# Low parts of the input weights by an accumulating DMA instead of a subtraction on GpSimd

## Chip, cores and metric

One core of a Trainium2 chip runs the whole program. The metric is the device time in microseconds; three runs of the kernel before took 576.79, 578.21 and 579.08 us, median 578.21.

## What is computed

The reference is one layer of a hybrid encoder on 1024 tokens of 1024 channels, float32:

```python
hn = rms_norm(h, ln_g)
proj = hn @ w_in + b_in                      # 1024 x 3584
glu_a, glu_b, z_conv, q, k, v, z_att = split(proj, 7 parts of 512)
y_conv = conformer_conv(glu_a, glu_b, ...)   # GLU, depthwise conv of width 31, LayerNorm, swish, pointwise
y_att = neighbourhood_attention(q, k, v, rpb)  # 8 heads of 64, 16 x 64 grid, window 8 x 16
y_conv = grouped_rms_norm(y_conv, gn_conv_g) * silu(z_conv)
y_att = grouped_rms_norm(y_att, gn_att_g) * silu(z_att)
out = rms_norm(h + concat(y_conv, y_att) @ w_out, final_g)
```

## The kernel before

Every large product is made from operands in two parts: the high part is the value rounded to float32r, the low part is what the rounding left. A product is then three matmuls, high by high, high by low and low by high (lines 384 to 386). For the input projection the weight is the stationary operand. It is cut into 28 chunks of 128 output channels; a chunk is one tile of 128 partitions by 8 parts (k) by 128 columns, 512 KB, and serves two halves of 512 tokens, 24 matmuls each.

`prefetch` (line 337) brings the chunks in the order of the work: the chunks of the GLU (b0, a0, b1, a1, b2, a2), then q0, k0, v0 make the lead (`LEAD`); the rest (`FILL`) is woven with the attention; the convolution gate's c3 and the attention gate's a3 come last, in `final_gates` (line 1033). For each chunk SyncE loads the raw weight into the one raw buffer (`wraw`, line 210); when one of two high/low buffer pairs is free, ScalarE copies the raw weight into `whi` in two pieces of four parts, which rounds it (line 351), and GpSimd subtracts: `wlo = raw - whi` (`low_weight`, line 355), also in two pieces. A pair is given back (`r_w.put`) when the second half of its chunk has been issued, so the pair of chunk n goes to chunk n + 2. The raw buffer is given back after the last subtraction.

All engines issue in the order in which this program was built. The class `Clock` plans that order: streams of work are generators that give the time from which they can go on, and queues of ScalarE, VectorE and GpSimd are booked with a cost for each instruction. Jobs for GpSimd wait in `ck.jobs` and are written when its booked queue is free (line 114). `proj` (line 368) takes a chunk's part k when its booked ready time has come, and other streams are taken meanwhile where they have work. In `final_gates` the products go part by part, c3 and then a3, so that every part lets go of its normalised input, whose buffers then take the output projection's operands.

VectorE works the 31 taps of the depthwise convolution through (`taps`, line 470), each a product and sum of two tiles in SBUF, and between them the low parts of q and k (`ql`, `kl`), which read the PSUM bank that the next projection needs. GpSimd has besides the subtractions the small powers of the norms and the attention's scalings, in order on one queue.

Of the kernel before, what the change touches and what calls it, by code (L numbers as in the profile page):

```python
# [32 lines left out]
CH_A, CH_B, CH_ZC, CH_Q, CH_K, CH_V, CH_ZA = 0, 4, 8, 12, 16, 20, 24  # L33
# rows of the small-vector tile
V_LN, V_BIN, V_DWB, V_CLG, V_CLB, V_GNC, V_GNA, V_N = 0, 8, 36, 40, 44, 48, 52, 56
# column blocks of 16 queries: (first 8-column granule, granules, bias class)
BLK = [(0, 3, 0), (1, 4, 1), (3, 4, 1), (5, 3, 2)]
BW = [24, 32, 24]
# row halves: (first key row, key rows)
HF = [(0, 11), (4, 12)]  # L40
# [30 lines left out]
class Ring:  # L71
    """the buffers of a tag, by the time from which each is free"""

# [16 lines left out]
class Clock:  # L90
    """Every engine issues in the order of this program. The work comes as streams, generators that give the
    time from which they can go on; they are woven by a clock of the tensor engine and of the others' queues."""

# [55 lines left out]
def block(ctx: ExitStack, tc: tile.TileContext, x, vecs, w_in, dw_w, pw_w, pw_b, rpb, w_out, final_g, out):  # L149
# [41 lines left out]

# [1 line left out]
    warm = const.tile([P, 1], F32, name="warm")  # L193
# [4 lines left out]

# [1 line left out]
    acc = yp.tile([P, NC4, T], F32, name="acc")  # L200
# [4 lines left out]

    # chunks of the projection in the order of the work: glu, q, k and v, gates of the attention and of the convolution
    of = {"g": (CH_B, CH_A), "q": (CH_Q,), "k": (CH_K, CH_V), "a": (CH_ZA,), "c": (CH_ZC,), "p": ()}
    order = [c + int(f[1:]) for f in LEAD + FILL for c in of[f[0]]] + [CH_ZC + 3, CH_ZA + 3]

    def wraw(n):  # L210
        c = order[n]
        raw = wrp.tile([P, NK, P], F32, tag="wr", name=f"wr{c}")
        nc.sync.dma_start(out=raw, in_=w_in[0][:, c * P:(c + 1) * P].rearrange("(k p) n -> p k n", p=P))
        return raw
# [66 lines left out]
    def turned(h):  # L281
        """first the banks of several chunks at a time, so that each tile of x is turned as it comes"""
        todo_ = list(range(NK))
        for group in ((("tr", "tr", "s", "s", "o", "ln"),) if h == 0 else ()) + (("tr",), ("s",)) * NK:
            ks, todo_ = todo_[:len(group)], todo_[len(group):]
            pts = []
            for k, tag in zip(ks, group):
                yield from RB[tag].get()
                pts.append((k, tag, bank(tag, f"px{h}_{k}", NB[tag])))
            for j in range(4):  # L290
                t = 4 * h + j
                while t not in x_ready:
                    yield ck.now + 0.1
                if x_ready[t] + ck.HOP > ck.now:
                    yield x_ready[t] + ck.HOP
                for k, tag, pt in pts:
                    ck.tp(pt[:, j * P:(j + 1) * P], xt[t][:, k * P:(k + 1) * P], ident)
                    if j == 3:
                        sl = slice(512 * h, 512 * h + 512)
                        e = ck.act(out=hi[k][:, sl], in_=pt, func=AF.Copy, scale=col(V_LN + k))  # L300
                        ck.spawn(low(h, k, pt, sl, e, RB[tag]), -1)
            yield
        for _ in range(4):
            r_u.put()
# [22 lines left out]

# [1 line left out]
    ready = {}  # L329

    def split(raw, whi, wlo, after=None, eng="pool"):
        """hi and lo of a weight; gives the time"""
        t = ck.act(after, out=whi, in_=raw, func=AF.Copy)
        k = dict(out=wlo, in0=raw, in1=whi.bitcast(F32), op=ALU.subtract)
        return ck.gps("tensor_tensor", 0.1 + 0.0022 * size(raw), t, **k) if eng == "pool" else ck.dve("tensor_tensor", t, **k)

    def prefetch():
        for n in range(len(order)):
            if n < W_AHEAD or "pw" in state:
                yield from r_raw.get()  # L340
                raw, end = (wraw(n), ck.now + 4.0) if n else (raw0, land_w)
                yield from r_w.get()
            else:
                yield from r_w.get()
                yield from r_raw.get()
                raw, end = wraw(n), ck.now + 4.0
            whi, wlo = wtiles(n)
            yield end
            for k0 in range(0, NK, KS):
                kk = slice(k0, k0 + KS)  # L350
                t = ck.act(out=whi[:, kk, :], in_=raw[:, kk, :], func=AF.Copy)
                ck.jobs.append((t, partial(low_weight, n, raw, whi, wlo, kk)))
                yield

    def low_weight(n, raw, whi, wlo, kk):
# [12 lines left out]
    def proj(w, h, name, order=None, tag="pj"):  # L368
        """one chunk of channels for half of the tokens; order: width of the column blocks
        that become the outer dimension of the tokens"""  # L370
        whi, wlo, wt = w
# [18 lines left out]

# [1 line left out]
    # CLS: first query row, first key row written, key rows, window by the row offsets -4..3  # L392
    CLS = ((0, 0, 8, False), (4, 0, 11, True), (8, 4, 12, True), (12, 8, 8, False))
# [3 lines left out]
    def bias_rows():  # L397
# [20 lines left out]
        r_gz.put()  # L418
        # a window that moves with the column: columns c0..c0+n, bias columns from 7 on
        for t, c0, n in ((0, 8, 8), (1, 0, 16), (2, 0, 9)):  # L420
            w = BW[t]
            for h in range(8):
# [3 lines left out]
                yield ck.now + 0.3  # L426
        # a window at the border
        for t, start, cs in ((0, 0, range(8)), (2, 8, range(9, 16))):
            for c in cs:
                nc.sync.dma_start(out=ab[t][:, c, :, start:start + 16], in_=rp8[:, :, 15 - c:31 - c])  # L430
                yield ck.now + 0.3
        # a row of mask before, and laid out for the query rows
        for t in range(3):
# [31 lines left out]

# [1 line left out]
    # a sigmoid is half of 1 + tanh of the half, and the taps carry the half  # L467
    u, conv_end = [], [0.0] * 8
# [21 lines left out]
    def all_taps():  # L490
        """two chunks in turn, so that a tap need not wait for the one before; the last chunk by halves of the tokens"""
        n = 0
# [45 lines left out]

# [1 line left out]
    pair = {}  # L540
# [46 lines left out]
    def q_out(i, q, pq, sl, bq):  # L587
        """q[0]: hi and lo of the first head; q[1]: lo and hi of the second"""
        tag, r = (("gz", r_gz), ("ul", r_ul))[sl.start > 0]
# [17 lines left out]
    def k_out(i, kh, kl, pk, sl, bk):  # L607
        """kh[a]: hi of a head, twice; kl: lo of both"""
        t = ck.act(out=kh[1][:, sl], in_=pk, func=AF.Identity, bias=bk)
# [33 lines left out]
    def group_scale(src, ms, sq, sums=None):  # L643
        """ms: (mean of squares over each 64 + eps * sums^2) ** -0.5; sq is scratch"""
        g = sq.rearrange("p (g d) -> p g d", d=64)
# [12 lines left out]

# [1 line left out]
    def grid(ap):  # L660
# [5 lines left out]
    def scores(n):  # L666
        """S of a block of 16 columns of a head, and its exponentials"""
        i, a, b = blocks[n]
# [49 lines left out]
    def attention():  # L718
        """the scores run a block ahead"""
        yield from scores(0)  # L720
# [90 lines left out]

# [1 line left out]
    pwh, pwl, ln_end, stage = [], [], {}, [0]  # L813
# [22 lines left out]
    def pointwise(t):  # L836
# [35 lines left out]
        yield from r_ul.get()  # L872
        # half: z / 2; silu(z) = z / 2 * (1 + tanh(z / 2))
        th = half_tile("ul", f"th{t}")
# [39 lines left out]

# [1 line left out]
    def y_ready(c, h):  # L916
# [11 lines left out]
    def gated(y, pz, c, h, banks):  # L928
        """y: half of what z = pz + bias gates; silu(z) = z / 2 * (1 + tanh(z / 2))"""
        yield from r_gz.get()  # L930
# [21 lines left out]

# [1 line left out]
    def work(items):  # L954
# [73 lines left out]
    last = {}  # L1028
    # the chunks of the output projection that come last
    LATE = (3, 7)  # L1030
    K_OUT = [k for k in range(NK) if k not in LATE] + list(LATE)

    def final_gates():
        """the last two chunks of gates, k by k: each lets go of its part of the normalised input"""
        ends = (CH_ZC + 3, CH_ZA + 3)
# [27 lines left out]

# [1 line left out]
    def split_y(t):  # L1065
# [57 lines left out]
    def pieces(t):  # L1123
        """columns of the products of a tile; the last ones are short"""
        ends = (0, 512, 768, 1024) if t == NT - 1 else (0, 512, 1024)
# [109 lines left out]
```

## Time and profile before

| | before |
|---|---|
| runs, us | 576.79, 578.21, 579.08 |
| profiled execution: span, us | 576.6 (its own time is not listed apart from the runs) |
| VectorE busy, us (share) | 414.7 (72%) |
| DMA moved | 54.58 MB, mean 95 GB/s |
| matmuls | 2717 |

A busy figure is the sum of an engine's instruction times within the span. For TensorE the ends of matmuls are modelled, so that neighbours overlap, and the distance between starts tells more than a duration. Chunks b and a of the GLU are `pb` and `pa` in the rows, q, k, v are `pq`, `pk`, `pv`, gates are `pz`; `wr`, `wh` and `wl` are raw, high and low weights. A row of the timeline gives the start, the time taken by one or by several merged instructions (xN), the engine, the line, the operation, what it writes and reads and, in brackets, the idle time before it with what ended it.

### The profile page before, as it was taken

What the parts mean: (1) busy time and instruction counts of PE and PEld (TensorE: products, weight loads), DVE (VectorE), ACT (ScalarE), POOL (GpSimd) and SP (SyncE); (2) the same over time, 40 slices, a digit from 0 to 9 for tenths busy, and PEclk for the clock granted to TensorE, in tenths of its full rate; (3) what the DMA queues carried; (4) which work ended last, traced back from release to release, by engine and by line L of the source; (5) the groups of instructions that cost most, each with busy time, mean ns of one, the idle gap of its engine ahead of it and who ended that gap; (6) DMA issues with size and microseconds to landing.
All of it is one profiled execution on the core that took longest, in us unless ns stands there. A gap on an engine that the chain in (4) does not pass through costs nothing.

```text
span 576.6 us, 7793 instructions
## 1 busy us (share of the span) xinstructions
PE 557.6 (97%) x2717; PEld 448.4 (78%) x2717; DVE 414.7 (72%) x665; ACT 259.7 (45%) x634; POOL 191.7 (33%) x176
## 2 busy tenths in 40 slices
PE   4999999899999999999999999999999999999995
PEld 3688887677878777777777877888888878888885
DVE  4747999999789988996899677756745265464232
ACT  5542221134554155544558455665755354253122
POOL 8413543241222331240524533642523353031121
PEclk9999999999999999999999999999999999999998
DMA  9413546652114422332232230120100580043221
GB/s 331 132 21 82 167 128 220 181 158 80 36 56 110 103 61 72 89 101 71 64 114 80 79 90 17 38 59 18 39 0 8 181 286 0 2 146 135 84 74 73
DMA packets 60410, 54.58 MB, mean 95 GB/s; under 512 B 9597, under 2 KB 51381, under 8 KB 60372
## 3 DMA queue, kind: packets, MB, share of 16 engines
q1 hardware_dynamic: 60302, 54.07, 31.0%
q8 instruction: 21, 0.34, 0.2%
q14 instruction: 17, 0.14, 0.1%
q10 hardware_dynamic: 70, 0.03, 0.0%
HBM read 36.58 MB, written 11.58 MB: 84 GB/s over the span
## 4 chain that ended last, share of the span: by engine, by line
PE 82%; DVE 12%; DMA 1%; ACT 1%; POOL 1%; SPq 1%; issue 1%; POOLq 0%; ACTq 0%; DVEq 0%
PE out L127 15%; PE pz L127 15%; DVE acc L140 10%; PE pv L127 8%; PE pk L127 7%; PE s L127 6%; PE pq L127 5%; PE ptp L131 5%; PE po L127 5%; PE pb L127 4%; PE pw L127 4%; PE pa L127 3%; PE po L131 1%; DMA x<-in_x 1%; PE px L131 1%; DVE x L140 1%
## 5 line engine op out<-in xcount | busy, mean ns | idle before, releaser
L140 DVE SCALAR_TENSOR_TENSOR acc<-glu,dwc,acc 128x512 f32<-128x512 f32 (+25 forms) x150 | 187.6, 1275 | 1.1
L144 POOL TENSOR_TENSOR wl<-wr,wh 128x512 fp32r<-128x512 f32 x56 | 89.1, 1610 | 133.1 <-ACT wh L136 127.9
L127 PE MATMUL pz<-hi,wh 128*128 128x512 f32 x128 | 52.3, 408 | 0.0
L127 PE MATMUL out<-wol,yh 128*128 128x512 f32 (+1 forms) x136 | 51.2, 377 | 0.0
L127 PE MATMUL out<-woh,yl 128*128 128x512 f32 (+1 forms) x136 | 51.2, 376 | 0.0
L127 PE MATMUL out<-woh,yh 128*128 128x512 f32 (+1 forms) x136 | 51.2, 376 | 0.0
L127 PE MATMUL pz<-hi,wl 128*128 128x512 f32 x128 | 50.3, 393 | 0.1
L127 PE MATMUL pz<-lo,wh 128*128 128x512 f32 x128 | 50.1, 391 | 0.0
L136 ACT ACTIVATE pth<-ptp 128x512 fp32r<-128x512 f32 x64 | 32.2, 544 | 32.2 <-PE ptp L131 32.2
L136 ACT ACTIVATE wh<-wr 128x512 fp32r<-128x512 f32 x56 | 32.3, 631 | 27.5 <-DMA wr<-in_w_in 14.2
L140 DVE TENSOR_TENSOR ptl<-ptp,pth 128x512 fp32r<-128x512 f32 x64 | 37.1, 614 | 1.7 <-ACT pth L136 1.3
L144 POOL TENSOR_TENSOR ams<-ams,mhalf 128x8 f32<-128x8 f32 x8 | 15.6, 1948 | 62.1 <-DVE ams L140 62.1
L140 DVE TENSOR_TENSOR xr<-out,xr 128x512 f32<-128x512 f32 (+1 forms) x17 | 11.1, 659 | 34.1 <-PE out L127 29.6
L136 ACT ACTIVATE prob<-s,mx 128x264 f32<-128x264 f32 (+1 forms) x64 | 33.7, 537 | 2.1 <-DVE mx L140 2.1
L131 PE MATMUL ptp<-ident,prob 128*128 128x128 f32 x224 | 32.0, 279 | 0.1
L140 DVE CUSTOM_DVE_ANT_0 s<-s,bias 128x264 f32<-128x264 f32 (+1 forms) x64 | 30.7, 507 | 1.6 <-PE s L127 0.7
L136 ACT ACTIVATE os<-po 128x256 f32<-128x256 f32 x32 | 12.4, 389 | 41.3 <-PE po L127 41.2
L127 PEld LDWEIGHTS out<-woh,yh 128*128 128x128 f32 x136 | 25.6, 188 | 4.8
L127 PEld LDWEIGHTS out<-woh,yl 128*128 128x128 f32 x136 | 25.6, 188 | 4.7
L127 PEld LDWEIGHTS out<-wol,yh 128*128 128x128 f32 x136 | 25.6, 188 | 4.6
L127 PE MATMUL po<-ptl,v 128*128 128x256 f32 x112 | 28.5, 284 | 0.5 <-DVE ptl L140 0.5
L131 PEld LDWEIGHTS ptp<-ident,prob 128*128 128x128 f32 x224 | 24.5, 140 | 5.7 <-issue 2.3
(153 smaller groups left out, 1380.7 us busy)
## 6 DMA issues: line engine op xcount, KB each, us to landing
wr<-in_w_in SPq DMA_DIRECT2D x28, 512.0 KB
x<-in_x SPq DMA_DIRECT2D x8, 512.0 KB
wor<-in_w_out SPq DMA_DIRECT2D x8, 512.0 KB
xr<-in_x SPq DMA_DIRECT2D x8, 512.0 KB
out<-xr SPq DMA_DIRECT2D x16, 256.0 KB
kh<-kh SPq DMA_DIRECT2D x24, 128.0 KB
q<-ql SPq DMA_DIRECT2D x16, 128.0 KB
row<-abn SPq DMA_DIRECT2D x16, 96.0 KB
```

The source lines that it names most:

```text
L127: self.nc.tensor.matmul(out, lhsT=lhsT, rhs=rhs, start=start, stop=stop)
L131: self.nc.tensor.transpose(out=out, in_=in_, identity=identity)
L136: self.nc.scalar.activation(**k)
L140: getattr(self.nc.vector, fn)(**k)
L144: getattr(self.nc.gpsimd, fn)(**k)
```

## The change

The weights are laid out on the host by chunks, so that a chunk is one contiguous array of 128 rows of 4 KB. The first chunk (n = 0) is made as before. For the others ScalarE makes the high part, gives back the raw buffer, then writes the negated high part into `wlo` with two more copies; GpSimd issues one DMA that reads the weight from HBM once more and adds it to what stands in `wlo`. All eight parts of such a chunk are booked ready at one time: 1.1 us of GpSimd's queue and 2.6 us more. Comments of the file were dropped too, which is left out here.

```diff
 def wraw(n):
     c = order[n]
     raw = wrp.tile([P, NK, P], F32, tag="wr", name=f"wr{c}")
-    nc.sync.dma_start(out=raw, in_=w_in[0][:, c * P:(c + 1) * P].rearrange("(k p) n -> p k n", p=P))
+    nc.sync.dma_start(out=raw, in_=w_in[c])
...
             whi, wlo = wtiles(n)
             yield end
+            if n == 0:
+                for k0 in range(0, NK, KS):
+                    kk = slice(k0, k0 + KS)
+                    t = ck.act(out=whi[:, kk, :], in_=raw[:, kk, :], func=AF.Copy)
+                    ck.jobs.append((t, partial(low_weight, n, raw, whi, wlo, kk)))
+                    yield
+                continue
             for k0 in range(0, NK, KS):
                 kk = slice(k0, k0 + KS)
                 t = ck.act(out=whi[:, kk, :], in_=raw[:, kk, :], func=AF.Copy)
-                ck.jobs.append((t, partial(low_weight, n, raw, whi, wlo, kk)))
                 yield
+            r_raw.put(t)
+            for k0 in range(0, NK, KS):
+                kk = slice(k0, k0 + KS)
+                t = ck.act(out=wlo[:, kk, :], in_=whi[:, kk, :].bitcast(F32), func=AF.Copy, scale=-1.0)
+                yield
+            ck.jobs.append((t, partial(low_added, n, whi, wlo)))
+
+    def low_added(n, whi, wlo):
+        nc.gpsimd.dma_start(out=wlo, in_=w_in[order[n]], accum_op=ALU.add)
+        t = max(ck.q["pool"], ck.now) + 1.1
+        ck.q["pool"] = t
+        ready[n] = (whi, wlo, [t + 2.6] * NK)
...
+    w_in = np.asarray(inputs["w_in"])[0].reshape(NK, P, -1, P).transpose(2, 1, 0, 3)
```

## Rows read from the trace of the kernel before

**Rows 1.** Page, part 1: busy us, share of the span, instructions

```profile
PE 557.6 (97%) x2717; PEld 448.4 (78%) x2717; DVE 414.7 (72%) x665; ACT 259.7 (45%) x634; POOL 191.7 (33%) x176
```

**Rows 2.** Timeline of TensorE: instructions with idle time before them

```profile
30.52 1.64 PE L131 MATMUL px<-ident,x 128*128 128x128 f32 x13 [0.47 <-DVE x L140]
...
102.04 0.49 PE L127 MATMUL pk<-hi,wh 128*128 128x512 f32 x1 [0.84 <-DVE ql L140]
...
109.43 0.50 PE L127 MATMUL pk<-hi,wh 128*128 128x512 f32 x1 [1.64 <-DVE ql L140]
```

**Rows 3.** Chain that ended last: start us, us, what

```profile
35.30 5.46 PE pb L127 x24
...
48.54 1.28 DVE acc L140
...
49.84 2.20 DVE acc L140
...
105.13 2.27 DMA q<-ql
```

**Rows 4.** Page, part 5: busy us, mean ns of one, idle before

```profile
L144 POOL TENSOR_TENSOR wl<-wr,wh 128x512 fp32r<-128x512 f32 x56 | 89.1, 1610 | 133.1 <-ACT wh L136 127.9
...
L136 ACT ACTIVATE wh<-wr 128x512 fp32r<-128x512 f32 x56 | 32.3, 631 | 27.5 <-DMA wr<-in_w_in 14.2
```

**Rows 5.** Timeline of GpSimd: the subtractions of chunk 3

```profile
49.18 4.00 POOL L144 TENSOR_TENSOR wl<-wr,wh 128x512 fp32r<-128x512 f32 x2 [4.56 <-ACT wh L136]
```

**Rows 6.** Timelines of SyncE's DMA issues and ScalarE: two loads and their users

```profile
54.52 0.41 SPq L213 DMA_DIRECT2D wr<-in_w_in  x1
...
58.36 1.15 ACT L136 ACTIVATE wh<-wr 128x512 fp32r<-128x512 f32 x2 [0.55 <-DMA wr<-in_w_in]
...
110.60 0.39 SPq L213 DMA_DIRECT2D wr<-in_w_in  x1
...
115.92 1.16 ACT L136 ACTIVATE wh<-wr 128x512 fp32r<-128x512 f32 x2 [7.40 <-DMA wr<-in_w_in]
```

**Rows 7.** Timeline of ScalarE: high parts of five chunks

```profile
21.57 1.14 ACT L136 ACTIVATE wh<-wr 128x512 fp32r<-128x512 f32 x2
...
41.38 1.14 ACT L136 ACTIVATE wh<-wr 128x512 fp32r<-128x512 f32 x2
...
306.35 1.14 ACT L136 ACTIVATE wh<-wr 128x512 fp32r<-128x512 f32 x2
...
441.86 1.15 ACT L136 ACTIVATE wh<-wr 128x512 fp32r<-128x512 f32 x2
...
460.53 1.15 ACT L136 ACTIVATE wh<-wr 128x512 fp32r<-128x512 f32 x2 [4.53 <-PE pz L127]
```

**Rows 8.** Timeline of TensorE: first matmul on these chunks' low parts

```profile
25.67 0.40 PE L127 MATMUL pa<-hi,wl 128*128 128x512 f32 x1
...
46.49 0.39 PE L127 MATMUL pb<-hi,wl 128*128 128x512 f32 x1
...
314.47 0.39 PE L127 MATMUL pk<-hi,wl 128*128 128x512 f32 x1
...
449.19 0.39 PE L127 MATMUL pz<-hi,wl 128*128 128x512 f32 x1
...
462.59 0.50 PE L127 MATMUL pz<-hi,wl 128*128 128x512 f32 x1
```

**Rows 9.** Stretches: busy us by engine, granted clock, DMA share, GB/s

```profile
458.00:460.00 2.00, 2.00 (x10) 1.67 (x9) 0.00 (x0) 0.00 (x0) 0.00 (x0) 1.00 1.00 387
...
466.00:468.00 2.00, 2.00 (x11) 1.65 (x10) 1.74 (x1) 1.57 (x4) 1.91 (x2) 1.00 0.92 369
```

**Rows 10.** Page, part 3: DMA queue, packets, MB, share of 16 engines

```profile
q1 hardware_dynamic: 60302, 54.07, 31.0%
...
q10 hardware_dynamic: 70, 0.03, 0.0%
```

**Rows 11.** Stretch after the last matmul, columns as in rows 9

```profile
573.00:575.00 2.00, 0.00 (x0) 0.00 (x0) 0.00 (x0) 0.20 (x1) 0.00 (x0) 0.56 0.58 221
```

More of the change, by code (lines that the diff above doesn't have):

```diff
@@ L1223 @@
     nc = bacc.Bacc("TRN2", target_bir_lowering=False, num_devices=1)
-    inputs = dict(inputs, vecs=np.concatenate([np.asarray(inputs[n])[0].reshape(-1, P) for n in _VECS]))
+    w_in = np.asarray(inputs["w_in"])[0].reshape(NK, P, -1, P).transpose(2, 1, 0, 3)
+    inputs = dict(inputs, w_in=w_in, vecs=np.concatenate([np.asarray(inputs[n])[0].reshape(-1, P) for n in _VECS]))
     arrays, args = {}, []
```

## Prediction

> **What bounds the kernel now.** I read the busy table first, then TensorE's own timeline for every place where it idles, then the chain of waits. The busy table gives TensorE 97% of the span, ScalarE 45%, GpSimd 33% [rows 1]. A share is only an average, so the timeline decides: between 31 us and 569 us TensorE stands idle by the profile at two places alone, 0.84 us at 102.04 and 1.64 us at 109.43, both times until VectorE has written ql; before them one wait of 0.47 us at 30.52 is the longest since the projections began [rows 2]. From the spacing of matmul starts a few stalls hidden under the modelled ends add about 2 us more. So TensorE issues almost without a hole, one chunk's half costs 24 matmuls in 5.46 us (a chunk 10.92 us) [rows 3], and two things follow. Work taken off GpSimd can give back no more than the holes it causes, some 3 us and at the very most 5. And any weight that comes late makes a new hole that nothing gives back, because TensorE's order is fixed when the program is built.
>
> **What it removes.** 54 of the 56 GpSimd subtractions, 1.61 us each: 87 us less on GpSimd; ScalarE instead makes 54 negated copies of the same shape as the existing rounding copies [rows 4]. A pair of those takes 1.15 us, so 27 pairs add 31 us to ScalarE's 259.7, which makes about 50% of the span. Neither engine bounds. VectorE gains: a tap takes 1.28 us alone and 2.20 us while a subtraction runs (49.18 to 53.18 covers the tap at 49.84) [rows 3, 5]. VectorE has taps almost without a break from 48.5 us, and the two ql waits at 102 and 109 are its backlog. With about nine pairs of subtractions in that stretch, each stretching two taps by 0.92, some 16 us of backlog goes, and with it both holes: with what precedes and follows them I take 2.8 us (bounds 0 and 5).
>
> **What it adds: a longer way to a weight.** Before: a buffer comes free, ScalarE rounds (1.15 us a chunk), GpSimd follows piece by piece, and the first half of the low part is enough to go on. After: rounding 1.15, negation 1.15, a hop of 0.1, then GpSimd issues one DMA, and all eight parts count as ready only when the whole has landed. Call D the time from GpSimd's start on that issue to landing. No accumulating DMA is in this trace. The nearest rows: a plain load of the same 512 KB, issued at 54.52, releases ScalarE at 58.36, 3.8 us; one beside other traffic 110.60 to 115.92, 5.3 us [rows 6]; a copy of 128 KB lands in 2.27 us [rows 3]. The planner in the code books 1.1 us of issue and 2.6 us to landing; that number sets the written order and is no measurement. Lower end 2.7 us: the small copy and an issue like SyncE's 0.4 [rows 6]. Upper end 11.7: an issue of 1.1 and twice the slow load, since the sum has to read two sources. I take 5.0, an issue of 1.1 and the quiet load of 3.8, because the added read stands against rows of 4 KB instead of 512 B.
>
> The Trainium skill (DMA: Bandwidth & Descriptors, section on the anatomy of one DMA from GpSimd) fits such a DMA as 2.0 us plus the bytes at 436 GB/s; for 512 KB that is an estimate of 3.2 us, shorter than the 3.8 the row shows for a plain load. By that figure with the same issue, D would be 4.3 and the sum below some 3 us smaller; the row is taken.
>
> **Where the longer way is not hidden.** From ScalarE's start on the high part a chunk now needs 2.4 + D = 7.4 us until its low part can be used. Against it stands the first matmul that reads the low part [rows 7, 8]:
> - Chunk 1 (glu): 21.57 to 25.67, 4.1 us. Late by 3.3. Before the second half of x is turned there is nothing else to multiply, except that the small wait there, 0.47 us [rows 2], goes into it: 2.8 us.
> - Chunk 2: 41.38 to 46.49, 5.1 us, since only half a chunk lies between. Late by 2.3.
> - In the rest of the lead a buffer's release and its use are a whole chunk apart, 10.92 us; after the release come at most 0.7 us of other ScalarE work, so 8.1 us: nothing lost, up to D = 7.8.
> - The last k chunk: 306.35 to 314.47, 8.1 us: nothing at D = 5.0, late beyond D = 5.7.
> - Gate chunk c2: 441.86 to 449.19, 7.3 us; late by 0.1, and up to 2.3 where the evictions that stood behind the rounding on ScalarE come before the negation. I take 1.0.
> - The last chunk, a3: its buffer comes free when c2 ends at 460.5; ScalarE starts at 460.53 and TensorE wants the low part at 462.59. Here the old way, in halves, was just in time. And its DMA would start at 462.9 into DMA engines that are full: 1.00 and 0.92 busy in the stretches at 458 and 466 us, with the loads of the output weights [rows 9]. I add 1.5 us to D there, 6.5 in all: lands at 469.4, late by 6.8. Nothing else is left for TensorE: the output projection's operands need the buffers that these very products set free.
>
> How long the last chunk waits depends on how two queues share the engines. Nearly all packets of the trace are on one queue [rows 10], so no row shows it. If the new DMA waited behind what is queued, it would land when the load lets up, at some 471 us: late by 8.4. The Trainium skill (same page, section on queues, rings and completion order) has each engine take turns between queues, packet by packet; by that rule the DMA gets its share at once, which is nearer to the 6.5.
>
> Elsewhere: the 54 negations stand ahead of evictions that TensorE needs. The rounding copies stand there now, 1.15 us a pair, and from 127 us on the profile shows no wait of TensorE behind them, because the planner gives attention and projection work in turn; the cover is there. I take 0.5 (bounds 0 and 3). The raw buffer comes free after the rounding instead of after the subtraction, and the loads have longer runs; the load is what ScalarE waits for at 58.36 and 115.92 [rows 6], but in the lead TensorE's use lies a chunk behind, so both are worth nothing (bounds 0 and 0.5 gained). GpSimd's queue: behind the issue, which now waits for the negation, stand the small powers of the norms; each waits up to 1.15 us longer for the negation, but no longer for 2.5 us of subtraction: nothing. SyncE's queue loses only waits. 14 MB more come from HBM, at the 350 GB/s of rows 9 about 40 us of traffic spread over the span: in D.
>
> **The clock.** TensorE's granted clock is 1.00 throughout; when its last matmul has ended (570 us) it is 0.56 in the stretch from 573 to 575 us [rows 11], on the way to the lower level, 1.2 GHz. A hole of 6.8 us is longer than that, so matmuls behind it may start at the lower level. In four such microseconds two are lost; I take 2.0 (bounds 0 and 4).
>
> **The sum.** 2.8 + 2.3 + 1.0 + 6.8 + 0.5 + 2.0 - 2.8 = 12.6 us. The profiled execution has a span of 576.6 us, so 589.2; the median of the runs, 578.2, lies 1.6 us above that span for what is around it, so 590.8.
>
> **Rivals.**
> 1. The DMA lands quickly: D = 2.7 everywhere. Then chunk 1 costs 0.5, the last chunk 3.0, the rest nothing, and the ql holes give 2.8: 578.2 + 0.7 = 578.9. For it: the small copy of rows 3. Against it: the loads of rows 6 are four times the size.
> 2. The addition is slow, D = 8. Chunk 1 costs 5.8, chunk 2 5.3, the k chunk 2.3, c2 4.0, six chunks of the lead 0.2 each, the last (9.5) 9.8, the clock 4.0, less 2.8: some 30 us, 608. For it: two sources and bias traffic beside it. At the upper end, D = 11.7, each chunk of the lead would cost 4 us and the sum passes 60.
> 3. Other side, faster: VectorE's relief outweighs. Place: the two ql waits and the hidden stalls behind taps, between 47 and 300 us; price up to -5 us. It decides below D = 2, where the last chunk costs 2.3 and the rest nothing: 578.2 + 2.3 - 5 = 575.5. For it: the taps' 2.20 against 1.28. Against: D would have to be under the copy of a quarter of the size.
> 4. The change doesn't do what it says: the builder, knowing the later time of each weight, weaves other matmuls into the gaps. That can be at c2, where attention ends, but at chunks 1, 2 and the last nothing else is ready. It would take 1 to 2 us off: 589.3, inside the forecast's own spread.
>
> **Chances.** Forecast with D between 3.3 and 7, 581 to 601 us: 0.70 (rival 4 within it). Rival 2: 0.15. Rival 1: 0.10. Rival 3: 0.05. About 0.5% (3 us) is what a measurement of this kernel can tell from no change. The range 578.5 to 607 leaves out rival 3, half of rival 1 and the upper part of rival 2. Faster 0.05, same 0.11 (rival 1 and the quickest of the forecast), slower 0.84.
>
> **What would show it.** After the change TensorE's timeline must have a wait of 2 to 4 us at the start of the second chunk (25 us), one of 1 to 4 us before the third, and one of 4 to 9 us some 20 us ahead of the output projection, each ended by the DMA into wl; taps of 2.20 us and the two ql waits must be gone; ScalarE near 291 us, GpSimd near 105 to 135 us. After the long hole the granted clock should dip. Wrong would be: landings within 3 us of issue, no hole at the last chunk, or TensorE's waits ending on something other than the low parts.

## The result and the profile after

The changed kernel took 606.76 us (median of four runs, 604.64 to 609.94) beside 578.22 (576.79 to 579.08) for the kernel before on the same chip: a ratio of 1.050, 95% interval 1.046 to 1.0541. So it is slower, as forecast, but by 28.5 us where 12.6 were forecast; the time lies at the upper end of the range. The profiled execution took 605.64 us, with a span of 603.4. Of the runs below, one execution of x14_last (601.14 us) is left out of its ratio as a slow one, being over 1.5% above the fastest of its kernel.

From the page after: busy time of each engine (us, share, instructions), granted clock in 40 slices, the DMA queues (packets, MB, share), the group that issues the new DMA, and the median from issue to landing.

```profile
PE 565.0 (94%) x2717; PEld 453.8 (75%) x2717; DVE 381.3 (63%) x665; ACT 288.3 (48%) x688; POOL 130.6 (22%) x149
...
PEclk9998999898999999999999999999999979999998
...
q1 hardware_dynamic: 35214, 54.07, 28.9%
q0 software_dynamic: 3888, 14.16, 13.7%
...
L369 POOL DMA_DIRECT2D wl<-in_w_in x27 | 24.4, 902 | 165.4 <-ACT wl L136 161.0
...
wl<-in_w_in POOLq DMA_DIRECT2D x27, 512.0 KB, 6.3
```

The engines came out as forecast: GpSimd 191.7 to 130.6 us, ScalarE 259.7 to 288.3, VectorE 414.7 to 381.3, a relief of 33 us [rows 1]. It bought almost nothing, since TensorE's idle rows show late weights instead. The timeline of TensorE, every wait over 0.2 us from the second half of x on:

```profile
27.32 0.33 PE L131 MATMUL px<-ident,x 128*128 128x128 f32 x1 [2.25 <-DVE x L140]
28.84 1.42 PE L131 MATMUL px<-ident,x 128*128 128x128 f32 x11 [1.19 <-DVE x L140]
32.46 0.47 PE L127 MATMUL pa<-hi,wl 128*128 128x512 f32 x1 [1.51 <-DMA wl<-in_w_in]
54.76 0.77 PE L127 MATMUL pb<-hi,wl 128*128 128x512 f32 x1 [3.94 <-DMA wl<-in_w_in]
114.35 0.47 PE L127 MATMUL pk<-hi,wl 128*128 128x512 f32 x1 [2.80 <-DMA wl<-in_w_in]
141.46 0.36 PE L127 MATMUL s<-kh,q 128*128 128x264 f32 x1 [3.31 <-DMA kh<-kh]
236.73 0.44 PE L131 MATMUL ptp<-ident,prob 128*128 128x128 f32 x2 [0.28 <-ACT ya L136]
238.16 0.48 PE L127 MATMUL pq<-hi,wh 128*128 128x512 f32 x1 [0.99 <-DVE v L140]
467.70 0.50 PE L127 MATMUL pz<-hi,wl 128*128 128x512 f32 x1 [0.59 <-DMA wl<-in_w_in]
479.98 0.47 PE L127 MATMUL pz<-hi,wl 128*128 128x512 f32 x1 [0.21 <-DMA wl<-in_w_in]
487.23 0.77 PE L127 MATMUL pz<-hi,wl 128*128 128x512 f32 x1 [5.62 <-DMA wl<-in_w_in]
```

In [rows 2] stood two waits for ql; both are gone. Five places now wait for a DMA: chunks 1 and 2, k0, the first scores and the last gates (three rows). What each cost is read by setting the start of the same matmul after against before: this difference, the shift, is constant where nothing is lost and steps where something is.

| place | shift behind it, us | step | forecast |
|---|---|---|---|
| chunk 1 (a0) | 4.2 | 4.2 | 2.8 |
| chunk 2 (b1) | 9.8 | 5.6 (hole 4.1, clock 1.5) | 2.3 |
| first k chunk, k0 | 11.5 | 1.6 (hole 2.8, clock 1.7, ql about -2.8) | -2.8 (ql alone) |
| chunk b3 and the first scores | 16.7 | 5.2 (hole 3.3, clock 1.6, the rest open) | 0 |
| from there to the last gate chunk | 18.6 | 1.9 | 1.5 |
| last chunk (a3) | 26.4 | 7.8 (hole 5.6, clock 1.8, the rest the small wait ahead) | 6.8 |

The forecast's 2.0 for the clock is one term beside these. What the clock cost is counted from the distance of matmul starts behind each hole, some 0.43 us instead of 0.23. The granted clock of stretches of 4 us, columns as in [rows 9]:

```profile
56.00:60.00 4.00, 4.00 (x15) 3.20 (x15) 3.89 (x4) 0.00 (x0) 0.00 (x0) 0.79 0.93 194
...
116.00:120.00 4.00, 4.00 (x13) 3.17 (x12) 0.81 (x1) 0.00 (x0) 0.00 (x0) 0.61 0.95 221
...
144.00:148.00 4.00, 4.00 (x16) 3.40 (x15) 3.62 (x5) 1.60 (x6) 0.00 (x0) 0.70 0.94 217
...
480.00:484.00 4.00, 1.61 (x6) 1.00 (x6) 1.63 (x3) 3.78 (x6) 1.94 (x2) 1.00 1.05 419
484.00:488.00 4.00, 0.77 (x2) 0.70 (x3) 2.68 (x1) 0.00 (x0) 1.59 (x1) 0.54 0.99 208
488.00:492.00 4.00, 4.00 (x12) 3.11 (x12) 1.17 (x4) 1.12 (x4) 0.00 (x0) 0.60 0.55 187
```

TensorE is busy through the first three of these stretches and issues 13 to 16 matmuls in them, where the kernel before issues 19 and 18 in the stretches at 56 and 116 us: part of each stretch ran at full speed (2.4 GHz), part at the lower level (1.2 GHz). At the last chunk the order is plain: 1.00 in the stretch in which the wait begins, 0.54 in that of the wait, 0.60 when work has begun again, and 1.00 from 492 us. This happened behind four holes, not one.

Two places were not on my list, and their causes stand in other engines' timelines. First the k0 chunk, on GpSimd's queue and on ScalarE:

```profile
92.27 0.85 POOL L369 DMA_DIRECT2D wl<-in_w_in  x1
105.32 0.42 POOL L144 MEMSET abn<- 128x384 f32 x1 [12.20 <-DMA row<-abn]
107.73 0.50 POOL L144 COPY abn<-abn 128x192 f32<-128x192 f32 x1 [1.99 <-DMA abn<-ab]
108.27 0.86 POOL L369 DMA_DIRECT2D wl<-in_w_in  x1
```

```profile
103.44 1.14 ACT L136 ACTIVATE wl<-wh 128x512 fp32r<-128x512 f32 x2
```

ScalarE has the negated copy ready at 104.6 us, yet the DMA is issued at 108.27, 3.7 us later: it is written behind a memset and a copy for the attention's bias table, which wait for DMAs of their own (12.20 and 1.99 us). Before, the subtraction of this chunk stood ahead of them. Second, the scores wait for kh, whose DMA copies land late. The chain of waits there and at the last chunk (start, us, what):

```profile
134.69 6.64 DMA kh<-kh
...
481.62 5.48 DMA wl<-in_w_in
```

### The profile page after: what moved, and what is told of

Same layout as the page of the kernel before. It is cut to its first block, busy times and chain, and to the rows that moved or that the text cites. A ratio compares the mean times of both kernels' runs of the same rounds, so it can differ in the third digit from the quotient of the medians.

```text
span 603.4 us, 7834 instructions
## 1 busy us (share of the span) xinstructions
PE 565.0 (94%) x2717; PEld 453.8 (75%) x2717; DVE 381.3 (63%) x665; ACT 288.3 (48%) x688; POOL 130.6 (22%) x149
## 3 DMA queue, kind: packets, MB, share of 16 engines
q0 software_dynamic: 3888, 14.16, 13.7%
## 4 chain that ended last, share of the span: by engine, by line
PE 85%; DMA 7%; issue 3%; ACT 2%; DVE 1%; SPq 0%; POOL 0%; POOLq 0%; DVEq 0%; ACTq 0%
PE out L127 14%; PE pz L127 12%; PE pk L127 7%; PE pb L127 7%; PE pv L127 7%; PE pa L127 7%; PE pq L127 7%; PE s L127 6%; DMA wl<-in_w_in 5%; PE ptp L131 4%; PE po L127 4%; PE pw L127 4%; DMA kh<-kh 1%; DMA x<-in_x 1%; PE po L131 1%
## 5 line engine op out<-in xcount | busy, mean ns | idle before, releaser
L140 DVE SCALAR_TENSOR_TENSOR acc<-glu,dwc,acc 128x512 f32<-128x512 f32 (+24 forms) x150 | 159.8, 1091 | 1.2
L369 POOL DMA_DIRECT2D wl<-in_w_in x27 | 24.4, 902 | 165.4 <-ACT wl L136 161.0
L140 DVE TENSOR_TENSOR ytok<-po,ytok 128x128 f32<-128x128 f32 x32 | 9.3, 290 | 42.7 <-ACT ytok L136 42.6
L127 PEld LDWEIGHTS pz<-hi,wl 128*128 128x128 f32 x128 | 24.6, 192 | 13.0 <-issue 6.0
L136 ACT ACTIVATE wl<-wh 128x512 fp32r<-128x512 f32 x54 | 30.8, 620 | 0.0
L127 PE MATMUL pb<-hi,wl 128*128 128x512 f32 x64 | 26.7, 417 | 3.9 <-DMA wl<-in_w_in 3.9
```

What stands on the lines that cost most here:

```text
L127: self.nc.tensor.matmul(out, lhsT=lhsT, rhs=rhs, start=start, stop=stop)
L136: self.nc.scalar.activation(**k)
L140: getattr(self.nc.vector, fn)(**k)
L369: nc.gpsimd.dma_start(out=wlo, in_=w_in[order[n]], accum_op=ALU.add)
```

## Experiments

Main theory (L): every chunk's way to its low part became longer than its slack; the price is the holes and the clock behind them. Rivals are named with each run. Before ran beside each at 577.7 to 578.2 us (medians).

**Layout alone (x1_layout).** All 28 chunks by subtraction, the new host layout kept.

```diff
-            if n == 0:
+            if True:
```

> The new layout of the weights alone: GpSimd subtracts for all 28 chunks, as before the change, no negation and no accumulating DMA. Theory L (the added time is the longer way to a low part, where the slack is short): 577 to 579, the layout is worth nothing, TensorE has no hole ended by wl. Rival T (load: what the change adds to the DMA engines' and ScalarE's work, and another order of the loads, costs): the layout lowers load, so 574 to 577; if the shorter loads disturb the written order, 580 or more.

578.94 us, ratio 1.0026 (1.0014 to 1.0039); no hole beyond those of [rows 2]. The layout loses about 1 us (2.3 at most by the interval); nearly all of the 28 us come of the rest of the change, the negations and the DMAs.

**The same DMA without the addition (x2_plain).** The kernel leaves the addition out, so its low parts hold the whole weight.

```diff
-        nc.gpsimd.dma_start(out=wlo, in_=w_in[order[n]], accum_op=ALU.add)
+        nc.gpsimd.dma_start(out=wlo, in_=w_in[order[n]])
```

> The changed kernel, but GpSimd's DMA writes the weight over the negated high part instead of adding to it, so the low parts hold the whole weight and the products are not the reference's. Same order, same bytes from HBM. If the addition makes the way long (theory L, with its price in the adding): the landing falls from 6.3 us to about 4.5, the four or five holes shrink by 1.8 us each, 595 to 599. If the length is in a DMA from GpSimd as such: landing 5.8 us or more, 603 to 607. Rival T expects 603 to 607 too, since the traffic hardly changes.

594.51 us, ratio 1.03 (1.0248 to 1.0353). The lines on wl of the two traces, first the changed kernel's, then this one's (us from issue to landing):

```profile
DMA to landing us min/median/max: 5.3/6.3/10.2
```

```profile
DMA to landing us min/median/max: 3.5/4.7/8.6
```

The page's line on the queue of these DMAs, beside the 13.7% above:

```profile
q0 software_dynamic: 3888, 14.16, 7.9%
```

And this kernel's waits of TensorE that answer to those above (the trace is that of its quickest run, 591.04 us):

```profile
51.57 0.47 PE L127 MATMUL pb<-hi,wl 128*128 128x512 f32 x1 [2.06 <-DMA wl<-in_w_in]
...
129.57 0.36 PE L127 MATMUL s<-kh,q 128*128 128x264 f32 x1 [0.77 <-DMA kh<-kh]
...
472.04 0.76 PE L127 MATMUL pz<-hi,wl 128*128 128x512 f32 x1 [5.58 <-DMA wl<-in_w_in]
```

The addition costs 1.6 us a landing, and without it 12 of the 28 us go: the hole at chunk 2 halves, k0's is gone, the scores' shrinks from 3.31 to 0.77. The packets are as many and as large, but their time falls from 13.7% to 7.9%: in the traces' records a packet of 4 KB takes 328 ns in the median with the addition and 174 ns without. With eight such packets on each of 16 engines that is an estimate of 1.2 us a DMA; the issue takes 0.3 us more (0.90 against 0.60). k0's hole did not go by its landing, which took 6.1 us here and 5.9 there: its DMA was issued 1.2 us behind the negation instead of 3.7, because the bias table's DMAs had come sooner. The forecast of 590.8, made with D = 5.0, comes near the time of this kernel.

**The tight chunks back to subtraction (x3_short).** Chunks 0, 1, 2 and 27.

```diff
-            if n == 0:
+            if n in (0, 1, 2, 27):
```

> The changed kernel with GpSimd's subtraction for chunks 1, 2 and 27 (the three with the least slack), accumulating DMAs for the other 24. Theory L: the three holes of 4.2, 5.6 and 7.4 us (clock included) go, the late k0 and the late scores stay: 586 to 592. Rival T: 24 of 27 DMAs and negations are still there, so the waits show up at other places: 598 or more.

592.34 us, ratio 1.025 (1.0213 to 1.0287). The three holes are gone, and others have come:

```profile
94.37 0.51 PE L127 MATMUL pq<-hi,wl 128*128 128x512 f32 x1 [2.59 <-DMA wl<-in_w_in]
132.65 0.36 PE L127 MATMUL s<-kh,q 128*128 128x264 f32 x1 [3.14 <-DMA kh<-kh]
```

At q0 the DMA, issued at 87.62, stands behind a bias-table copy (86.73), that of the table's second part; k0's stood behind the third. The time is just above the forecast of L: the three tight chunks are worth 14 us, not the 17.6 of their steps.

**Only the last chunk back (x14_last).**

```diff
-            if n == 0:
+            if n in (0, 27):
```

> As the changed kernel, but the last chunk too by GpSimd's subtraction. Theory A (the last hole with the clock behind it is a term by itself): 7.8 us off, 597 to 601 us, the shift to the kernel before unchanged up to the last gate chunk. Rival B (the ring of two buffer pairs and the builder's order pass the cost on): less than 4 us off, 603 us or more.

595.57 us (591.63 to 598.29), ratio 1.0302 (1.0246 to 1.0358): 11.2 below the changed kernel, more than the 7.8 of the step and just under theory A's range. The trace is that of the 601.14 us; in it the shift is 22 us ahead of the last chunk, where the changed kernel's was 18.6, and it stays there through the chunk. The last hole is a term by itself; its size by this run is uncertain by some microseconds.

**ScalarE's negations kept, GpSimd subtracts (x4_neg_sub).** No DMA adds; the negated copy is overwritten.

```diff
-            r_raw.put(t)
...
-            ck.jobs.append((t, partial(low_added, n, whi, wlo)))
+            for k0 in range(0, NK, KS):
+                ck.jobs.append((t, partial(low_weight, n, raw, whi, wlo, slice(k0, k0 + KS))))
```

> ScalarE's 54 negated copies kept, but GpSimd then subtracts over them as before and no DMA adds: ScalarE's share of the change alone. Theory L: the way is 1.15 us longer, which shows at chunk 1 (0.7) and at the last (1.2), perhaps 1.5 more elsewhere: 579 to 583. Rival T, if ScalarE's 31 us are what delays the evictions: 588 or more.

591.36 us, ratio 1.024 (1.0216 to 1.0264). A miss for L: a longer way costs this without any DMA behind it. TensorE's largest wait is

```profile
118.07 0.80 PE L127 MATMUL pv<-hi,wl 128*128 128x512 f32 x1 [3.81 <-POOL wl L144]
```

at v0, whose raw weight was asked for at 106.50 us only and was still being waited for by ScalarE up to 111.70: the raw buffer is now held until behind the negation. That is not the whole of it: k0's subtraction ended at 102.6, and the load then stood behind SyncE's copies for the bias table and q; and k0's rounding is itself written later, at 96.79 against 90.34 in the kernel before. About 7 us more go between 145 and 460 us.

**k0's DMA ahead of the bias table (x7_bias_behind).** The bias stream is held back so that the DMA is written first.

```diff
+            if t == 2:
+                yield ck.now + 6.0
             yield from r_y.get()
```

> The changed kernel; the planner takes up the third part of the bias table 6 us later, so that on GpSimd's queue the DMA of chunk k0 stands ahead of the table's memset and copy, which wait for SyncE's DMAs, and no longer behind them. Theory G (k0's hole of 2.8 us at 114 us, with the lower clock behind it, comes of that order on GpSimd's queue): the hole goes, 601 to 604. Rival (k0 is late because raw weight and DMA are late in the traffic): the hole stays within 1 us of 2.8, 605 to 608.

604.11 us, ratio 1.0462 (1.0424 to 1.0499), at the top of theory G's range; the interval overlaps the changed kernel's, so the place tells more than the total. The wait at k0 fell from 2.80 to 0.91 us, its step from +1.6 to -1.9. So GpSimd's order made most of that hole. Chunks 1 and 2 came out 2.2 us dearer in the profiled execution: there the first matmul on a0 took 0.77 us instead of 0.47, and the granted clock from 32 to 36 us was 0.50, in the changed kernel's trace 1.00.

**Chunk b3 by subtraction (x11_b3).**

```diff
-            if n == 0:
+            if n in (0, 9):
```

> The changed kernel with GpSimd's subtraction for chunk 9 (b3) alone besides chunk 0. Its negations stand on ScalarE ahead of k's last eviction, and its DMA runs beside SyncE's copies of k that the first scores wait for. Theory S (these two make the hole of 3.3 us before the scores, with the lower clock behind it): the hole falls below 1 us, 601 to 604. Rival (the copies are late through SyncE's queue and the bias table's traffic): the hole stays at 2.5 us or more, 605 to 608.

603.48 us, ratio 1.0433 (1.0386 to 1.0481), as theory S had it, though this interval too overlaps the changed kernel's. The scores wait for kh no more; instead

```profile
144.89 0.43 PE L127 MATMUL s<-kh,q 128*128 128x352 f32 x1 [1.57 <-ACT prob L136]
...
485.56 0.77 PE L127 MATMUL pz<-hi,wl 128*128 128x512 f32 x1 [6.24 <-DMA wl<-in_w_in]
```

and the step of this place is 2.4 instead of 5.2. b3's preparation is the cause of that wait: in the changed kernel ScalarE's rounding and negation stand ahead of kh's copy (126.47 and 127.53, then 128.57), and the weight's DMA (128.96) beside kh's (130.06 and 134.13). Which of the two weighs more was not told apart.

**The negated copy first (x8_neg_first).** `wlo` is written from the raw weight before `whi`, so the DMA can start 1.15 us earlier, with the same instructions.

```diff
-                t = ck.act(out=whi[:, kk, :], in_=raw[:, kk, :], func=AF.Copy)
...
+                t = ck.act(out=wlo[:, kk, :], in_=raw[:, kk, :], func=AF.Copy, scale=-1.0)
+                yield
+            ck.jobs.append((t, partial(low_added, n, whi, wlo)))
...
+                t = ck.act(out=whi[:, kk, :], in_=raw[:, kk, :], func=AF.Copy)
```

> The changed kernel with ScalarE's two copies exchanged: the negated high part is made first, straight from the raw weight, and the high part while the DMA runs. Same instructions, same traffic; the way to a low part is 1.15 us shorter. Theory L: each of the five holes shrinks by about 1.15 us and some of the lower clock goes with them: 597 to 601. Rival T (traffic and ScalarE's load): 604 to 608.

610.91 us, ratio 1.0572 (1.054 to 1.0603): both theories missed. The hole at chunk 2 did shrink by the 1.1 us (3.94 to 2.86), but others grew:

```profile
54.47 0.80 PE L127 MATMUL pb<-hi,wl 128*128 128x512 f32 x1 [2.86 <-DMA wl<-in_w_in]
114.96 0.50 PE L127 MATMUL pk<-hi,wl 128*128 128x512 f32 x1 [3.76 <-DMA wl<-in_w_in]
...
362.55 0.36 PE L127 MATMUL s<-kh,q 128*128 128x264 f32 x1 [2.75 <-DMA kh<-kh]
...
492.72 0.80 PE L127 MATMUL pz<-hi,wl 128*128 128x512 f32 x1 [7.60 <-DMA wl<-in_w_in]
```

The last DMA took 8.56 us here against 5.48. SyncE's loads of the output weights and of x for the residual were issued from 473.85 to 480 us, the last 4 us before it; in the changed kernel they are out by 472, 10 us before it. In the traces' records of DMA packets SyncE's queue fills the engines behind the issue in both; the first packet of the weight's DMA comes 4.3 us after its issue here and 2.1 there.

**Two DMAs of half a chunk (x9_halves).**

```diff
-        nc.gpsimd.dma_start(out=wlo, in_=w_in[order[n]], accum_op=ALU.add)
+        for k0 in range(0, NK, KS):
+            kk = slice(k0, k0 + KS)
+            nc.gpsimd.dma_start(out=wlo[:, kk, :], in_=w_in[order[n]][:, kk, :], accum_op=ALU.add)
```

> The changed kernel with the accumulating DMA in two halves of 256 KB, issued one behind the other; the parts are still booked ready together. If the landing of 6.3 us is mostly a fixed time, the first half lands no sooner than about 5 us and the second at 7: the holes keep their size, 605 to 610. If it is mostly in the bytes, the first half lands at 3.5 to 4 us, TensorE goes on with four parts, and the holes lose 2 us each: 596 to 601.

601.97 us, ratio 1.0427 (1.0406 to 1.0448), between the two forecasts. The landings, both halves together:

```profile
DMA to landing us min/median/max: 3.8/5.8/10.7
```

The median mixes two kinds: the first half lands 5.1 us after its issue, the second, which queues behind it, 6.3 after its own and 7.0 after the first's. So half the bytes come 1.2 us sooner than the whole did, and the whole 0.7 later; the wait at chunk 2 is 2.40 instead of 3.94 and k0's is gone, the scores' (3.16) and the last chunk's (6.37) are not.

**The true landing booked (x6_late_booking).** No work changes, only the times that the builder plans with.

```diff
-        t = max(ck.q["pool"], ck.now) + 1.1
+        t = max(ck.q["pool"], ck.now) + 0.9
...
-        ready[n] = (whi, wlo, [t + 2.6] * NK)
+        ready[n] = (whi, wlo, [t + 5.4] * NK)
```

> The changed kernel with the planner's booking set to what the trace shows, 0.9 us of issue and 5.4 to landing, in place of 1.1 and 2.6: the written order then knows the length of the way. Theory L: chunks 1, 2 and the last have nothing to put in between, their holes stay (together 15 to 18 us with the clock); k0 and the scores may be given other work: 600 to 606. Rival B (the wrong booking is the cause): most holes go, 590 or less.

613.02 us (604.53 to 613.28), ratio 1.0569 (1.049 to 1.0648). A builder that knows the landing weaves nothing useful into the gaps, and the order that it writes is no better (the interval overlaps the changed kernel's): a wait of 2.51 us at q0 and one of 2.80 at scores at 216 us are new. My fourth rival is out as a cure. At chunk 1, though, the changed kernel's own order had done what it says: turns of x (27.32 and 28.84 us in the rows above) stand ahead of the late products, and stood behind the first of them before.

**Only three chunks of the lead (x10_mid).** 3 to 5, where the slack is a whole chunk.

```diff
-            if n == 0:
+            if n not in (3, 4, 5):
```

> Accumulating DMAs for chunks 3, 4 and 5 alone (a1, b2, a2), GpSimd's subtraction for the rest. Their slack is a whole chunk, so theory L expects no hole from them, and three pairs of subtractions less beside VectorE's taps, about 5 us of its backlog: one or both ql waits go, 575 to 578. Rival T: traffic from three DMAs beside the bias table delays it, 579 to 582.

577.30 us (12 runs), ratio 0.9991 (0.9975 to 1.0006): no change that can be told. The two ql waits are gone here too, against one wait

```profile
69.55 0.50 PE L127 MATMUL pb<-hi,wl 128*128 128x512 f32 x1 [1.13 <-DMA wl<-in_w_in]
```

At its place the relief of VectorE is as large as forecast: the shift is 1.4 us ahead of the two waits and -1.6 behind them, 3.0 gained. That wait and one of 0.44 us at the scores take most of it back. This is the best version found; no version beat the kernel before.

**The fill alone (x5_lead).** Chunks 11 to 26 by the DMA, all others by subtraction.

```diff
-            if n == 0:
+            if n < 11 or n == 27:
```

> GpSimd's subtraction for chunks 0 to 10 and 27, accumulating DMAs for the 16 chunks between, which are woven with the attention. Theory L: slack there is 8 us or more, and only what the ScalarE copies delay is left: 579 to 583, and the two ql waits of the kernel before are back. Rival T: 16 of 27 DMAs and negations cost their share, 590 or more.

591.9 us, ratio 1.0255 (1.0231 to 1.0278): L missed. Up to q1 the matmuls start where they did before; 12 of the 13.8 us go near the last k chunk, with these rows of TensorE and of ScalarE:

```profile
315.90 0.58 PE L127 MATMUL po<-pth,v 128*128 128x256 f32 x1 [2.36 <-ACT pth L136]
319.93 0.58 PE L127 MATMUL po<-ptl,v 128*128 128x256 f32 x1 [3.46 <-DVE ptl L140]
```

```profile
312.99 1.17 ACT L136 ACTIVATE wh<-wr 128x512 fp32r<-128x512 f32 x2
314.02 1.17 ACT L136 ACTIVATE wl<-wh 128x512 fp32r<-128x512 f32 x2
315.06 0.30 ACT L136 ACTIVATE ytok<-po 128x128 f32<-128x128 f32 x1
315.22 0.63 ACT L136 ACTIVATE pth<-ptp 128x512 fp32r<-128x512 f32 x1
```

The first of the two is behind ScalarE, where the rounding and negation are written ahead of ytok and pth, which the attention needs; neither is for a weight. Together they are 5.8 us, and behind them the granted clock is 0.50 from 316 to 324 us. The second ends with VectorE's ptl, whose lateness was not followed further. In the changed kernel the same chunk's rounding (321.28) stands behind a pth (315.97), and nothing is lost.

**The fill alone, negated by GpSimd (x12_pool_neg).** To take ScalarE's part away.

```diff
-            if n == 0:
+            if n < 11 or n == 27:
...
-            for k0 in range(0, NK, KS):
-                kk = slice(k0, k0 + KS)
-                t = ck.act(out=wlo[:, kk, :], in_=whi[:, kk, :].bitcast(F32), func=AF.Copy, scale=-1.0)
-                yield
...
+        for k0 in range(0, NK, KS):
+            kk = slice(k0, k0 + KS)
+            ck.gps("tensor_scalar", 0.65, out=wlo[:, kk, :], in0=whi[:, kk, :].bitcast(F32), scalar1=-1.0, scalar2=None, op0=ALU.mult)
         nc.gpsimd.dma_start(out=wlo, in_=w_in[order[n]], accum_op=ALU.add)
```

> As x5_lead (accumulating DMAs only for the 16 chunks woven with the attention), but GpSimd makes the negated copies, so ScalarE has no more to do than before the change. Theory A (what x5_lead lost, 13.8 us, is the negations ahead of evictions on ScalarE where it is full, around 310 us): 577 to 581. Rival D (it is the DMA's length and traffic, or the other order of the work): 588 or more.

594.18 us, ratio 1.0294 (1.0275 to 1.0313), in rival D's range. Theory A is not settled by it: no wait of the kind that x5_lead had at 315 us is left, but the two negations take 3.15 us on GpSimd, the way is longer again, and now the weight is late, at the chunk whose slack I had put at 8.1 us:

```profile
318.72 0.76 PE L127 MATMUL pk<-hi,wl 128*128 128x512 f32 x1 [4.63 <-DMA wl<-in_w_in]
```

**Half of the fill (x15_second_half).** Chunks 19 to 26 alone by the DMA.

```diff
-            if n == 0:
+            if n < 19 or n == 27:
```

> Only the eight chunks 19 to 26 (the last k and v chunks, then gates) by the accumulating DMA. Where all sixteen chunks of the fill were so made, 12 of 13.8 us were lost by the last k chunk. Theory A (that chunk alone loses it, since ScalarE's rounding and negation there stand ahead of the copies that the attention needs): 588 to 592 us with holes at about 315 us. Rival B (it is gathered on the way through the eight chunks before): 578 to 583 us, no hole over 1.5 us at 315 us.

582.64 us, ratio 1.0086 (1.0064 to 1.0108). Rival B had it: the same last k chunk, fed by the same DMA, waits nowhere at 315 us; the largest wait is 1.71 us, at scores at 346 us. So the 12 us do not belong to that chunk's DMA by itself. ScalarE's order around it differs too: ytok (313.80) stands ahead of the rounding (313.96) here, and behind the negation in x5_lead.

**The lead and the last chunk alone (x13_lead_acc).** The fill back to subtraction.

```diff
-            if n == 0:
+            if n == 0 or 10 < n < 27:
```

> Lead chunks (1 to 10) and the last one by the accumulating DMA, the first and the sixteen of the fill (11 to 26) by GpSimd's subtraction. The fill's sixteen by the DMA alone cost 13.8 us; in the changed kernel TensorE loses only 1.9 us between the scores and the last gate chunk. Theory A (the costs of the places add up, and the changed kernel's fill is cheap only by the order that the builder wrote there): 606.8 less 13.8, 591 to 596 us, the lead's holes unchanged and the fill gaining time against the kernel before. Rival B (the fill's cost is hidden once the lead is late, since VectorE and ScalarE got ahead in the lead's holes): 606.8 less 1.9, 603 to 606 us, holes of the lead and the last chunk as in the changed kernel, none between 145 and 460 us.

609.34 us, ratio 1.055 (1.0516 to 1.0583). Theory A is refuted: taking the fill's sixteen DMAs away gives back none of the 13.8 us. As rival B had it, there is no wait over 0.5 us between 145 and 460 us (the shift goes from 19.7 to 20.4), but the total is above B's 603 to 606, because chunk 1 came out 2.3 us dearer with the clock down, as in x7_bias_behind, and the last chunk waited longer. TensorE's row, and then the chain's:

```profile
493.10 0.77 PE L127 MATMUL pz<-hi,wl 128*128 128x512 f32 x1 [10.25 <-DMA wl<-in_w_in]
```

```profile
483.39 9.57 DMA wl<-in_w_in
```

Here, as in x8_neg_first, SyncE's loads of the output weights run close ahead of that DMA and beside it (475.02 to 477.7, two more at 487.40); SyncE's queue fills the engines, and the first packet of the weight comes 4.9 us after the issue. That loads ahead of it lengthen the last landing is read from three traces (5.48, 8.56, 9.57 us) and from the chunk before it in the changed kernel, whose DMA was issued at 469.61 among these loads and took 10.23; no run moved the loads alone.

## Why the prediction was right or wrong

**What bounds it: right.** TensorE's order is fixed, and each late weight opened a hole that nothing gave back. The relief of GpSimd and VectorE was worth the two ql waits and no more: 3.0 us at their place in x10_mid, against 2.8 forecast, and no measurable gain in its total. (One short wait was overlooked, 0.50 us for ptl at 291.52.)

**D = 5.0: this step failed first.** The landing was 6.3 us in the median, 5.3 at best and 10.2 at worst. The reason given for 5.0, that 4 KB rows make up for the added read, fails: x2_plain has the same rows without the addition at 4.7, and the addition puts 1.6 on top. With each chunk's own landing the prediction's formula holds at chunk 2 (2.4 + 6.6 - 5.1 = 3.9 us; the wait was 3.94) and at the last chunk (5.5 makes it 5.8; 5.62). At chunk 1 it does not: that landing took 8.1 us, which makes 2.4 + 8.1 - 4.1 - 0.5 = 5.9, and 4.2 was lost, with the turns of x written ahead. That the median of 6.3 would make 4.1 there is chance. The Trainium skill (DMA: Bandwidth & Descriptors, section on the anatomy of one DMA from GpSimd) led to an estimate of 3.2 us for 512 KB; without the addition the quickest landing, 3.5 us, is near that, but the median of 4.7 is not, and neither is any landing with the addition.

**"In the rest of the lead ... nothing lost, up to D = 7.8": failed, and not by D.** k0 and the scores cost 1.6 and 5.2 us, where the forecast had the ql waits' -2.8 for the whole stretch. I asked what is queued behind GpSimd's issue, but not what the issue is queued behind: the bias table's memset and copy, 3.7 us (x7_bias_behind puts them behind, and most of the hole goes). And I counted only whether a weight is late, not what its preparation delays: b3's negation and DMA against kh's (x11_b3). The prediction's "so 8.1 us" for this stretch is a slip: 10.92 less 0.7 is 10.2, from which its 7.8 follows; the landings there were 5.7 to 8.2 us.

**The clock, 2.0 once: mis-sized.** 1.5, 1.7, 1.6 and 1.8 us were lost behind four holes of 2.80 to 5.62 us, 6.6 in all. No row stood behind the four microseconds that its 2.0 goes by; the size for one hole came out near, the number of holes did not. In the traces of x7_bias_behind, x11_b3, x13_lead_acc and x14_last the clock was down at chunk 1 as well.

**The last chunk: near, with one term wrong.** 7.8 us with its clock, against 6.8 and a clock of 2.0. The 1.5 us for the loads of the output weights were not paid there: the landing took 5.5, less than the median. They were paid by the chunk before. The trace's record of DMA packets shows that DMA, issued at 469.61, without a packet for 4.6 us, while SyncE's queue filled the engines (1.01 busy); it landed at 479.84, when TensorE had just come to need it (a wait of 0.21). The Trainium skill (DMA: Bandwidth & Descriptors, section on queues, rings and completion order) has each engine take turns between queues, packet by packet; the trace does not agree for those 4.6 us, and agrees with it behind them, when the two queues had 0.54 and 0.51 of the engines. The last DMA had its first packet 2.1 us after its issue, when SyncE's loads ran out, and then the engines nearly alone. Why a first packet comes so late is not shown.

**The fill and c2: 1.5 forecast, 1.9 measured, but for no good reason.** "The cover is there" is false as a property of the change: alone, the same sixteen chunks cost 13.8 us (x5_lead), eight of them 4.5, and x4_neg_sub, with no DMA that adds, about 7. In the changed kernel undoing them gains nothing (x13_lead_acc). What differs between these traces is the order that the builder writes around each chunk; x6_late_booking changes that order and no work, and new waits came with it (2.51 and 2.80 us). That the order is the cause is argued from these rows, at the last k chunk above all (x5_lead against x15_second_half); no run changed the order there alone. Which rule of the builder puts ScalarE's copies ahead of the attention's at one place and behind them at another stays open.

Of the rivals, the second (slow addition, 608 us at D = 8) came nearest in time, with another makeup: D was 6.3, and k0, the scores and the clock made the rest; that the time lies near is chance.

## What to carry to other kernels

When a step's way to its data gets longer, list for each use the slack, and then look at both sides of the queue: what the new instruction waits behind, and whose work it stands ahead of. Time a DMA by its landing in this program's traffic, with whatever it does besides moving bytes, and read the granted clock behind every hole rather than counting it once. In a program with a written order, costs of places do not add up: try the parts alone and together before trusting a sum.

## What the runs showed of the hardware

- An accumulating DMA of 512 KB, issued by GpSimd, landed 5.3 to 10.2 us after its issue (median 6.3); the same without the addition 3.5 to 8.6 (4.7). Its issue holds GpSimd for 0.90 us in the mean against 0.60, and a packet of 4 KB takes 328 ns in the median against 174.
- Where SyncE's queue filled the engines at 0.92 or more behind the issue, the first packet of such a DMA came 2.1 to 4.9 us after the issue (changed kernel, x8_neg_first, x13_lead_acc); at most other places of the changed kernel 1.6 to 2.2.
- Of two DMAs of 256 KB with addition, issued one behind the other, the first landed in 5.1 us in the median, the second 7.0 us after the first's issue, against 6.3 for one of 512 KB.
- The same written order came out two ways at the start: the first matmul on a0 took 0.47 us in the changed kernel's profiled execution and 0.77 or 0.76 in those of x7_bias_behind, x11_b3, x13_lead_acc and x14_last. The granted clock from 32 to 36 us was 1.00 in the first and 0.50 or 0.51 in the others, and the shift behind chunk 1 was 4.2 us in the first and 5.7 to 6.5 in the others.
